# Modulation products of a two-block network: from TensorE column tiles to VectorE running sums

## The chip, the cores and the metric

One core of a Trainium2 chip. The metric is device time in microseconds (us) of one execution. Engines are named as in the profile: PE is TensorE (PEld its weight loads), DVE VectorE, ACT ScalarE, POOL GpSimd, SP the engine that issues the DMAs.

## The reference

Two transformer-like blocks of two layers each work on 256 context tokens and 256 latent tokens with 1024 features. Each layer l has a *modulation*: six vectors of 1024 numbers (shift, scale and gate for each half of the layer) for each of two conditions, c for the latent tokens and c_ctx for the context.

```python
def _modulation(cond, w, b):          # cond [1, 1024], w [1024, 6144]
    m = jax.nn.silu(cond) @ w + b
    return jnp.split(m[:, None, :], 6, axis=-1)

ml = _modulation(c, ada_w[i], ada_b[i])
mc = _modulation(c_ctx[None, :], ada_w[i], ada_b[i])
...
hl = _modulate(x, ml[0], ml[1])       # x * (1 + scale) + shift, latent tokens
...
x = _layer_norm(ALPHA * x + ml[2] * yl, ln_g[i, 0], ln_b[i, 0])
```

The context's stream ends in the last layer of each block, so that there only shift and scale of the first half (parts 0 and 1) are wanted for both conditions, and parts 2 to 5 for the latent condition alone. All data is fp32.

## The kernel before

Features lie on the 128 partitions and tokens in the columns. A projection takes its weights in chunks of 128x1024 fp32 (512 KB): `weight` (L266) loads a chunk into one of five buffers `raw`, ScalarE rounds it to `wh` (L280), VectorE, or GpSimd for each third chunk, subtracts to get the rest `wl` (L281), with three buffers for each of the two; `mm3` (L284) then issues three products for every 128x128 block (L286 to L288), of 512 columns where both halves of the tokens are worked on and of 256 where one is.

The program runs: first mixer (`_mlstm`), first feed-forward block (`_ffn`), attention mixer on the latent tokens (`_mla`), second feed-forward block, then the second block's mixers (`_mixers`) and MLPs (`_mlp`), twice. Between two of these stands a norm: `resid` (L478) adds the last products to the stream, `accumulate` gathers sums (L486 to L503), `token_sums` (L312) sums over partitions on TensorE, and `ln_stats`, `ln_rows`, `rsqrt` and `rows` (L512, L343, L344, L322 to L328, L352) make the statistics by a chain of small VectorE instructions of two to eight columns; L908 and L909 (or L928) then normalise tile by tile, and `split` (L263, L264) makes the pairs for the next products. In the stages with both halves of the tokens (`front`) the first products of the first half run while the second half's norm is made.

The modulations are not computed ahead, but in the background. `ada(l)` (L398) is a generator whose step loads one weight chunk and multiplies it; `later` (L431) queues it with a rate, and `tick` (L435), called by each `weight`, lets it do that many steps per weight chunk; `finish` (L446) runs what is left where the results are needed. Layer 0's last four parts run beside the first mixer, layer 1's and 2's beside the first feed-forward block and the attention mixer, layer 3's beside the first MLP: 22 parts of eight chunks, 176 in all. (Parts 0 and 1 of layer 0 have their own code, `first_mod`, at the start.)

A chunk holds 128 input features (partitions) by 1024 outputs. The conditions `cs` are the stationary operand, 128x32 of which two columns are not zero, and the chunk is the moving one, as four column tiles of 256 outputs side by side, summed over the eight chunks in one PSUM bank:

```python
for j in range(4):
    nc.tensor.matmul(ps[32 * j:32 * j + 32, 0:256], self.cs[:, l // 2, kt, :],
                     raw[:, j, :], start=(kt == 0), stop=(kt == KD - 1),
                     tile_position=(0, 32 * j))
```

Each of these fp32 products leaves two records in the trace, so a chunk is eight records of L411. After the eighth chunk ScalarE copies the bank (L417), TensorE transposes two blocks (L420) and VectorE adds the bias (L425).

The order in which each engine does its instructions is set when the program is built: a scheduler that keeps a timeline of its own places them, by their order in the code and by when it takes each to be ready. On the chip every engine works through its list in that order.

## Time and profile before

| | |
|---|---|
| Median of 3 runs | 2565.69 us (2559.06 to 2566.53) |
| Span of the profiled execution | 2551.4 us |
| PE busy | 2467.2 us, 97% |
| DVE busy | 1330.9 us, 52% |
| ACT busy | 1089.1 us, 43% |
| POOL busy | 629.9 us, 25% |

The span runs from the first to the last instruction of the profiled execution. That execution has no other time of its own on record; the runs are other executions, and their median lies 14.3 us above the span. Busy time is the time in which an engine had an instruction at work, overlaps counted once. Idle time of an engine costs nothing unless another waits for it.

### The profile page before, as it was taken

What the parts mean: (1) busy time and instruction counts of PE and PEld (TensorE: products, weight loads), DVE (VectorE), ACT (ScalarE), POOL (GpSimd) and SP (SyncE); (2) the same over time, 40 slices, a digit from 0 to 9 for tenths busy, and PEclk for the clock granted to TensorE, in tenths of its full rate; (3) what the DMA queues carried; (4) which work ended last, traced back from release to release, by engine and by line L of the source; (5) the groups of instructions that cost most, each with busy time, mean ns of one, the idle gap of its engine ahead of it and who ended that gap; (6) DMA issues with size and microseconds to landing.
All of it is one profiled execution on the core that took longest, in us unless ns stands there. A gap on an engine that the chain in (4) does not pass through costs nothing.

```text
span 2551.4 us, 38440 instructions
## 1 busy us (share of the span) xinstructions
PE 2467.2 (97%) x15258; PEld 2079.0 (81%) x15258; DVE 1330.9 (52%) x2412; ACT 1089.1 (43%) x1861; POOL 629.9 (25%) x447
## 2 busy tenths in 40 slices
PE   7999999999999999999999999899999999988998
PEld 5777877888898777778878999668877778977998
DVE  4613333533645333346766566886633334597665
ACT  4733233422434223235545556664522323475543
POOL 1111222221452111124022322542111112252222
PEclk9999999999999999999999999999999999998999
DMA  8555434533324455556357553123445555223554
GB/s 287 185 181 162 123 117 135 158 96 115 107 99 143 148 158 156 164 176 213 103 166 240 177 172 123 54 83 96 129 153 157 156 157 165 67 87 108 179 177 125
DMA packets 114758, 369.84 MB, mean 145 GB/s; under 512 B 12689, under 2 KB 17041, under 8 KB 114577
## 3 DMA queue, kind: packets, MB, share of 16 engines
q1 hardware_dynamic: 114576, 367.37, 45.7%
q8 instruction: 120, 1.97, 0.3%
q14 instruction: 62, 0.50, 0.1%
HBM read 357.88 MB, written 9.44 MB: 144 GB/s over the span
## 4 chain that ended last, share of the span: by engine, by line
PE 88%; DVE 6%; ACT 3%; DMA 2%; issue 1%; SPq 0%; POOL 0%; DVEq 0%; ACTq 0%
PE pm L286 24%; PE pm L288 23%; PE pm L287 23%; PE px L286 4%; PE pa L411 4%; PE px L287 4%; PE px L288 4%; DVE a L1395 1%; DVE wl L281 1%; DMA raw<-in_ada 1%; PE px L312 1%; PE pm L1137 1%; PE px L336 1%; ACT wh L280 0%; DVE a L264 0%
## 5 line engine op out<-in xcount | busy, mean ns | idle before, releaser
L286 PE MATMUL pm<-a,wh 128*128 128x512 f32 (+1 forms) x2432 | 847.3, 350 | 8.8 <-ACT a L263 3.0
L287 PE MATMUL pm<-a,wh 128*128 128x512 f32 (+1 forms) x2432 | 835.7, 344 | 0.0
L288 PE MATMUL pm<-a,wl 128*128 128x512 f32 (+1 forms) x2432 | 833.0, 344 | 0.8 <-DVE wl L281 0.7
L280 ACT CAST wh<-raw 128x1024 fp32r<-128x1024 f32 (+2 forms) x421 | 420.0, 1001 | 844.1 <-PE pm L287 471.3
L281 POOL TENSOR_TENSOR wl<-raw,wh 128x1024 fp32r<-128x1024 f32 (+2 forms) x140 | 321.7, 2298 | 1472.3 <-ACT wh L280 1434.8
L286 PEld LDWEIGHTS pm<-a,wh 128*128 128x128 f32 x2432 | 462.3, 191 | 103.4 <-issue 34.6
L281 DVE TENSOR_TENSOR wl<-raw,wh 128x1024 fp32r<-128x1024 f32 (+2 forms) x281 | 342.7, 1221 | 363.2 <-ACT wh L280 360.3
L288 PEld LDWEIGHTS pm<-a,wl 128*128 128x128 f32 x2432 | 461.8, 190 | 56.3 <-DVE wl L281 1.3
L287 PEld LDWEIGHTS pm<-a,wh 128*128 128x128 f32 x2432 | 463.4, 191 | 50.5 <-DVE a L909 0.8
L286 PE MATMUL pm<-a,a 128*128 128x256 f32 (+2 forms) x844 | 245.8, 298 | 6.8 <-ACT a L280 6.8
L287 PE MATMUL pm<-a,a 128*128 128x256 f32 (+2 forms) x844 | 247.6, 295 | 2.5 <-DVE a L264 1.6
L288 PE MATMUL pm<-a,a 128*128 128x256 f32 (+2 forms) x844 | 246.2, 294 | 0.0
L286 PEld LDWEIGHTS pm<-a,a 128*128 128x128 f32 x844 | 162.7, 195 | 17.0 <-ACT a L280 8.3
L478 DVE SCALAR_TENSOR_TENSOR a<-pm,mod,a 128x256 f32<-128x256 f32 x188 | 87.4, 480 | 164.3 <-PE pm L288 163.9
L287 PEld LDWEIGHTS pm<-a,a 128*128 128x128 f32 x844 | 163.9, 194 | 6.8 <-DVE a L264 2.2
L288 PEld LDWEIGHTS pm<-a,a 128*128 128x128 f32 x844 | 163.9, 194 | 3.3 <-issue 1.4
L263 ACT CAST a<-t 128x256 fp32r<-128x256 f32 (+2 forms) x173 | 86.3, 506 | 123.9 <-DVE t L1699 82.0
L264 DVE TENSOR_TENSOR a<-t,a 128x256 fp32r<-128x256 f32 (+2 forms) x173 | 110.1, 642 | 53.0 <-ACT a L263 51.2
L287 PE MATMUL pm<-wl,a 128*128 128x512 f32 (+1 forms) x336 | 130.2, 388 | 5.1 <-DVE wl L281 5.1
L286 PE MATMUL pm<-wh,a 128*128 128x512 f32 (+1 forms) x336 | 128.0, 383 | 1.5 <-ACT a L263 1.5
L288 PE MATMUL pm<-wh,a 128*128 128x512 f32 (+1 forms) x336 | 127.6, 386 | 0.0
L286 PE MATMUL px<-a,wh 128*128 128x256 f32 (+1 forms) x364 | 122.2, 337 | 0.0
(305 smaller groups left out, 3325.0 us busy)
## 6 DMA issues: line engine op xcount, KB each, us to landing
raw<-in_ada SPq DMA_DIRECT2D x192, 512.0 KB, 4.2
raw<-in_w_m SPq DMA_DIRECT2D x128, 512.0 KB, 3.6
raw<-in_ffn_in SPq DMA_DIRECT2D x88, 512.0 KB, 4.1
raw<-in_w_qk SPq DMA_DIRECT2D x32, 512.0 KB, 3.6
raw<-in_w_v SPq DMA_DIRECT2D x32, 512.0 KB, 3.6
raw<-in_ffn_oa SPq DMA_DIRECT2D x32, 512.0 KB, 4.1
raw<-in_w_inb SPq DMA_DIRECT2D x28, 512.0 KB, 3.6
raw<-in_w_up SPq DMA_DIRECT2D x16, 512.0 KB, 5.8
```

The costliest lines, as they stand in the source:

```text
L263: self.nc.scalar.copy(hi, src)
L264: self.nc.vector.tensor_sub(lo, src, hi.bitcast(F32))
L280: nc.scalar.copy(hi, raw)
L281: eng.tensor_sub(lo, raw, hi.bitcast(F32))
L286: mm(out, ah, bh, start=start, stop=False)
L287: mm(out, ah, bl, start=False, stop=False)
L288: mm(out, al, bh, start=False, stop=stop)
L312: self.nc.tensor.matmul(out_ps[:, i * nt + t:i * nt + t + 1], a[:, c0 + t * P:c0 + (t + 1) * P], self.ones[:, 0:1], start=(k == 0), stop=( ...
L336: self.nc.tensor.transpose(ps[:, t * P:(t + 1) * P], col[:, t:t + 1].to_broadcast([P, P]), self.ident)
L411: nc.tensor.matmul(ps[32 * j:32 * j + 32, 0:256], self.cs[:, l // 2, kt, :], raw[:, j, :], start=(kt == 0), stop=(kt == KD - 1), tile_posi ...
L478: self.nc.vector.scalar_tensor_tensor(z[:, a:b], ps[:, a:b], gate[:, kt, w:w + 1], z[:, a:b], op0=ALU.mult, op1=ALU.add)
L1137: nc.tensor.transpose(pt[:, s * P:(s + 1) * P], p[:, s * P:(s + 1) * P], K.ident)
```

## The change

`ada` no longer multiplies on TensorE chunk by chunk. It keeps, for each condition, an accumulator of 128x1024 fp32 in SBUF (from the activations' pool, which has 31 such buffers). Each chunk is multiplied by the condition's value on each partition and added: the first by ScalarE, the other seven by VectorE, once per condition. For parts 2 to 5 of layers 1 and 3 only the latent condition is summed, which makes 14 parts with two conditions and 8 with one. After the eighth chunk TensorE sums each accumulator over the partitions, by products with a matrix of ones on column tiles of 512 columns; then follow the copy, now four transposes instead of two, and the bias. The rate of layer 0's parts rises from 0.5 to 0.8 steps per weight chunk.

```diff
-    def ada(self, l, parts=range(6), mod=None):
+    def ada(self, l, parts=range(6)):
...
+        if l % 2:
+            nc.gpsimd.memset(mod, 0.0)
         yield mod
         bo = _PV["ada_b"][0] + 48 * l
         for part in parts:
-            ps = self.pa.tile([P, 512], F32, name=self.uid("pa"), tag="pa")
+            conds = (1,) if l % 2 and part > 1 else (0, 1)
+            nw = len(conds)
+            acc = [self.a4(F32, (P, D)) for _ in conds]
             for kt in range(KD):
-                raw = self.rawp.tile([P, 4, 256], F32, name=self.uid("raw"), tag="raw")
-                nc.sync.dma_start(raw, self.A["ada"][6 * l + part - 2, kt])
-                for j in range(4):
-                    nc.tensor.matmul(ps[32 * j:32 * j + 32, 0:256], self.cs[:, l // 2, kt, :],
-                                     raw[:, j, :], start=(kt == 0), stop=(kt == KD - 1),
-                                     tile_position=(0, 32 * j))
+                raw = self.rawp.tile([P, D], F32, name=self.uid("raw"), tag="raw")
+                nc.sync.dma_start(raw, self.A["ada"][6 * l + part - 2, kt].rearrange("p a b -> p (a b)"))
+                for s, w in zip(acc, conds):
+                    c = self.cs[:, l // 2, kt, w:w + 1]
+                    if kt == 0:
+                        nc.scalar.activation(s, raw, AF.Copy, scale=c)
+                    else:
+                        nc.vector.scalar_tensor_tensor(s, raw, c, s, op0=ALU.mult, op1=ALU.add)
                 if kt < KD - 1:
                     yield
+            ng = 32 * 2 * nw
+            ps = self.pa.tile([P, 512], F32, name=self.uid("pa"), tag="pa")
+            for i in range(2 * nw):
+                nc.tensor.matmul(ps[32 * i:32 * i + 32], self.ones[:, 0:32],
+                                 acc[i // 2][:, 512 * (i % 2):512 * (i % 2) + 512],
+                                 start=True, stop=True, tile_position=(0, 32 * i))
             rows = self.t2()
-            nc.scalar.copy(rows[:, 0:256], ps[:, 0:256])
+            nc.scalar.copy(rows[0:ng], ps[0:ng])
             pt = self.ax_ps()
-            for h in range(2):
-                nc.tensor.transpose(pt[:, h * P:(h + 1) * P], rows[:, h * P:(h + 1) * P], self.ident)
+            for t in range(4):
+                nc.tensor.transpose(pt[:, t * P:t * P + ng], rows[0:ng, t * P:(t + 1) * P], self.ident[0:ng, 0:ng])
...
-    K.later(rest, 0.5)
+    K.later(rest, 0.8)
```

The rest of the difference adds the bias by the new layout of the transposed block and takes comments out. Lines behind `ada` are 13 higher in the new program.

The new instructions move others, since the scheduler places all of them anew. Two places on VectorE's list matter below; every row there is one instruction, with its line, operation, output and inputs. The first is the norm at the start of the first feed-forward block, second half of the tokens, from the sums' scaling (`st`, L512) to the end of its statistics (L352). Before (`px` is the bank with the sums, `v` and `rs` the small tiles of the norm, `t` and `pm` hidden tiles and products of the feed-forward block):

```order
L512 TENSOR_SCALAR st_6006<-px_5997 128x4
L343 SCALAR_TENSOR_TENSOR v_6008<-st_6006 128x2
L344 SCALAR_TENSOR_TENSOR v_6008<-v_6008,st_6006 128x2
L322 TENSOR_SCALAR rs_6011<-v_6008 128x2
L365 SCALAR_TENSOR_TENSOR t_6197<-pm_6147,pv,t_6197 128x255
L323 TENSOR_TENSOR rs_6011<-rs_6011 128x2
L367 SCALAR_TENSOR_TENSOR t_6197<-pm_6147,pv,t_6197 128x255
L324 SCALAR_TENSOR_TENSOR rs_6011<-rs_6011,v_6008 128x2
L325 SCALAR_TENSOR_TENSOR rs_6011<-rs_6011 128x2
L326 SCALAR_TENSOR_TENSOR rs_6011<-rs_6011 128x2
L327 SCALAR_TENSOR_TENSOR rs_6011<-rs_6011 128x2
L328 SCALAR_TENSOR_TENSOR rs_6011<-rs_6011 128x2
```

With the change (L525 is L512 of before; `a_6056` and `a_6057` are accumulators of two conditions, `raw` the chunk, `cs` the conditions):

```order
L525 TENSOR_SCALAR st_5974<-px_5965 128x4
L281 TENSOR_TENSOR a_6093<-raw_6090,a_6092 128x1024
L420 SCALAR_TENSOR_TENSOR a_6056<-raw_6094,cs,a_6056 128x1024
L420 SCALAR_TENSOR_TENSOR a_6057<-raw_6094,cs,a_6057 128x1024
L365 SCALAR_TENSOR_TENSOR t_6163<-pm_6113,pv,t_6163 128x255
L343 SCALAR_TENSOR_TENSOR v_5976<-st_5974 128x2
L420 SCALAR_TENSOR_TENSOR a_6056<-raw_6104,cs,a_6056 128x1024
L420 SCALAR_TENSOR_TENSOR a_6057<-raw_6104,cs,a_6057 128x1024
L367 SCALAR_TENSOR_TENSOR t_6163<-pm_6113,pv,t_6163 128x255
L344 SCALAR_TENSOR_TENSOR v_5976<-v_5976,st_5974 128x2
L281 TENSOR_TENSOR wl_6465<-raw_6462,wh_6464 128x1024
L365 SCALAR_TENSOR_TENSOR t_6221<-pm_6171,pv,t_6221 128x255
```

Two additions stand behind the scaling and before each further step of the chain; ten of them lie between L525 and the norm's last statistic, which stands some rows further down, and a subtraction of a weight chunk (L281) that stood behind the norm now lies in it.

The second place is the norm at the end of the attention mixer, which has one half of the tokens only. Before:

```order
L512 TENSOR_SCALAR st_11154<-px_11141 128x4
L343 SCALAR_TENSOR_TENSOR v_11156<-st_11154 128x2
L344 SCALAR_TENSOR_TENSOR v_11156<-v_11156,st_11154 128x2
L322 TENSOR_SCALAR rs_11159<-v_11156 128x2
L323 TENSOR_TENSOR rs_11159<-rs_11159 128x2
L324 SCALAR_TENSOR_TENSOR rs_11159<-rs_11159,v_11156 128x2
L325 SCALAR_TENSOR_TENSOR rs_11159<-rs_11159 128x2
L326 SCALAR_TENSOR_TENSOR rs_11159<-rs_11159 128x2
L281 TENSOR_TENSOR wl_11325<-raw_11322,wh_11324 128x1024
L327 SCALAR_TENSOR_TENSOR rs_11159<-rs_11159 128x2
L328 SCALAR_TENSOR_TENSOR rs_11159<-rs_11159 128x2
L352 TENSOR_TENSOR st_11154<-st_11154,rs_11159 128x2
```

With the change:

```order
L525 TENSOR_SCALAR st_10994<-px_10981 128x4
L281 TENSOR_TENSOR wl_11155<-raw_11152,wh_11154 128x1024
L420 SCALAR_TENSOR_TENSOR a_10957<-raw_11156,cs,a_10957 128x1024
L420 SCALAR_TENSOR_TENSOR a_10958<-raw_11156,cs,a_10958 128x1024
L343 SCALAR_TENSOR_TENSOR v_10996<-st_10994 128x2
L420 SCALAR_TENSOR_TENSOR a_10957<-raw_11160,cs,a_10957 128x1024
L420 SCALAR_TENSOR_TENSOR a_10958<-raw_11160,cs,a_10958 128x1024
L344 SCALAR_TENSOR_TENSOR v_10996<-v_10996,st_10994 128x2
L420 SCALAR_TENSOR_TENSOR a_10957<-raw_11170,cs,a_10957 128x1024
L420 SCALAR_TENSOR_TENSOR a_10958<-raw_11170,cs,a_10958 128x1024
L322 TENSOR_SCALAR rs_10999<-v_10996 128x2
L420 SCALAR_TENSOR_TENSOR a_10957<-raw_11239,cs,a_10957 128x1024
```

Here, too, ten additions lie between the scaling and the last statistic, where one subtraction stood. From the second half's norm before the attention mixer to its first softmax (L1124 before, L1137 now) the list holds 28 additions, between that softmax and the last but one head none, and from there to the end of the norm just shown 28.

## Rows read from the trace of the kernel before

**Rows 1.** page, busy time by engine and the chain that ended last

```profile
PE 2467.2 (97%) x15258; PEld 2079.0 (81%) x15258; DVE 1330.9 (52%) x2412; ACT 1089.1 (43%) x1861; POOL 629.9 (25%) x447
...
PE 88%; DVE 6%; ACT 3%; DMA 2%; issue 1%; SPq 0%; POOL 0%; DVEq 0%; ACTq 0%
```

**Rows 2.** windows, L411 alone: stretch, width, busy us (records) of PE, PEld, clock, DMA

```profile
64.00:740.00 676.00, 21.87 (x256) 5.64 (x256) 1.00 0.45 136
740.00:1080.00 340.00, 26.66 (x344) 8.29 (x344) 1.00 0.47 147
1080.00:1400.00 320.00, 35.15 (x432) 10.19 (x424) 0.98 0.54 180
1400.00:2200.00 800.00, 30.05 (x384) 7.85 (x384) 0.98 0.43 133
1160.00:1250.00 90.00, 11.69 (x144) 3.57 (x144) 1.00 0.58 199
1290.00:1350.00 60.00, 9.84 (x96) 2.28 (x96) 0.89 0.66 215
```

**Rows 3.** timeline of PE around one chunk: start us, us, instruction

```profile
111.21 0.39 PE L287 MATMUL pm<-a,wh 128*128 128x512 f32 x1
111.44 0.39 PE L288 MATMUL pm<-a,wl 128*128 128x512 f32 x1
111.75 0.64 PE L411 MATMUL pa<-raw,cs 128*32 128x256 f32 x8
...
112.66 0.39 PE L287 MATMUL pm<-a,wh 128*128 128x512 f32 x1
```

**Rows 4.** timeline of PE around two chunks in a row

```profile
1102.81 0.39 PE L288 MATMUL pm<-a,wl 128*128 128x512 f32 x1
1103.12 1.07 PE L411 MATMUL pa<-raw,cs 128*32 128x256 f32 x16
...
1104.47 0.40 PE L287 MATMUL pm<-a,wh 128*128 128x512 f32 x1
```

**Rows 5.** timeline of PE around the two transposes of a part

```profile
164.40 0.39 PE L288 MATMUL pm<-a,wl 128*128 128x512 f32 x1
...
165.08 0.39 PE L287 MATMUL pm<-a,wh 128*128 128x512 f32 x1
```

**Rows 6.** groups by line: DVE L365 (min/median/max ns), L281, L1395, ACT L280 (busy, mean)

```profile
L365 DVE SCALAR_TENSOR_TENSOR t<-pm,pv,t x60: 471/742/750, 69.2 to 1526.5; 128x510 f32<-128x510 f32 x32, 128x255 f32<-128x255 f32 x28
...
L281 DVE TENSOR_TENSOR a<-raw,a 128x1024 fp32r<-128x1024 f32 x34 | 50.1, 1480 | 11.7 <-ACT a L280 10.5 <-issue 0.5 <-DMA hf<-in_xT 0.5
...
L1395 DVE SCALAR_TENSOR_TENSOR a<-a,pv,a 128x512 f32<-128x512 f32 x30 | 32.3, 1088 | 0.2
...
L280 ACT CAST wh<-raw 128x1024 fp32r<-128x1024 f32 (+2 forms) x421 | 420.0, 1001 | 844.1 <-PE pm L287 471.3
```

**Rows 7.** timeline of DVE at the first feed-forward block's norm

```profile
767.47 0.16 DVE L512 TENSOR_SCALAR st<-px 128x4 f32<-128x4 f32 x1
...
771.89 0.16 DVE L352 TENSOR_TENSOR st<-st,rs 128x2 f32<-128x2 f32 x1
771.97 1.23 DVE L281 TENSOR_TENSOR wl<-raw,wh 128x1024 fp32r<-128x1024 f32 x1
773.11 0.42 DVE L1061 TENSOR_TENSOR t<-t,pm 128x256 f32<-128x256 f32 x1
```

**Rows 8.** windows, all engines: busy us (records) of PE, PEld, DVE, ACT, POOL, clock

```profile
1600.00:1664.00 64.00, 52.60 (x235) 40.59 (x235) 61.05 (x83) 38.62 (x70) 35.77 (x21) 0.89 0.22 74
...
1160.00:1250.00 90.00, 87.96 (x697) 74.91 (x696) 65.76 (x160) 53.07 (x110) 29.44 (x26) 1.00 0.58 199
...
1290.00:1350.00 60.00, 54.66 (x419) 43.98 (x418) 40.78 (x90) 30.58 (x64) 23.98 (x25) 0.89 0.66 215
...
768.00:788.00 20.00, 20.00 (x168) 19.09 (x161) 19.37 (x46) 15.61 (x29) 10.28 (x10) 1.00 0.59 196
1790.00:1810.00 20.00, 16.75 (x126) 15.20 (x127) 19.14 (x37) 17.27 (x35) 5.26 (x3) 0.91 0.74 252
```

More of the change, by code (lines that the diff above doesn't have):

```diff
@@ L395, in first_mod @@
                                     op0=ALU.add, op1=ALU.add)
-    def ada(self, l, parts=range(6), mod=None):
+    def ada(self, l, parts=range(6)):
         nc = self.nc
-        if mod is None:
-            mod = self.cp.tile([P, 6, KD, 2], F32, name=f"mod{l}", tag=f"mod{l}")
+        mod = self.cp.tile([P, 6, KD, 2], F32, name=f"mod{l}", tag=f"mod{l}")
+        if l % 2:
+            nc.gpsimd.memset(mod, 0.0)
         yield mod
@@ L418, in ada @@
             pt = self.ax_ps()
-            for h in range(2):
-                nc.tensor.transpose(pt[:, h * P:(h + 1) * P], rows[:, h * P:(h + 1) * P], self.ident)
-            m = mod[:, part].rearrange("p (j h) w -> p h j w", h=2)
-            b = self.pv[:, bo + part * KD:bo + (part + 1) * KD].rearrange("p (j h) -> p h j", h=2)
-            t = pt[:, 0:256].rearrange("p (h j w) -> p h j w", h=2, j=4)
-            for h in range(2):
-                nc.vector.tensor_tensor(m[:, h], t[:, h, :, 0:2],
-                                        b[:, h].unsqueeze(2).to_broadcast([P, 4, 2]), op=ALU.add)
+            for t in range(4):
+                nc.tensor.transpose(pt[:, t * P:t * P + ng], rows[0:ng, t * P:(t + 1) * P], self.ident[0:ng, 0:ng])
@@ L427, in ada @@
+            m = mod[:, part].rearrange("p (h t) w -> p w h t", h=2)
+            b = self.pv[:, bo + part * KD:bo + (part + 1) * KD].rearrange("p (h t) -> p h t", h=2)
+            t = pt.rearrange("p (t w h c) -> p w h t c", t=4, w=2, h=2)
+            for i, w in enumerate(conds):
+                nc.vector.tensor_tensor(m[:, w], t[:, i, :, :, 0], b, op=ALU.add)
             if part in (1, 4):
```

## The prediction

> **What bounds the kernel now.** I read the page first: TensorE is busy for 97% of a span of 2551.4 us and holds 88% of the chain that ended last, VectorE 6% [rows 1]. The reader should see that a microsecond taken from TensorE's queue shortens the span wherever nothing else is late, and that VectorE, at 52% overall, has room on average. An average says nothing of a stage, so I next cut the span into stages and counted the modulation products (records of L411, eight to a weight chunk) in each: 32 chunks beside the first mixer, 43 in the first feed-forward block, 54 from its end through the attention mixer into the second feed-forward block (one of them is cut by the boundary and counted twice), 48 in the last MLP stage that has them [rows 2]. Then the timeline of TensorE around single chunks [rows 3 to 5], because overlapping records make the busy time of a group less than what it costs. Last the busy time of VectorE in the stretches where the new order puts the added work [rows 8].
>
> **What TensorE loses and gains.** Products of L287 and L288 start 0.23 us apart. With one chunk between them L287 starts at 112.66 instead of about 111.90 [rows 3]: a chunk costs 0.77 us, more than the 0.57 us until the next product starts. Two chunks in a row cost 104.47 - 103.27 = 1.20 us, so the second adds 0.43 us [rows 4]. TensorE's order before has 155 groups: 113 of one chunk (87 us), 23 of two (28 us), and 19 pieces that hold the other 17 chunks (13 us at 0.77). Together **128 us, 0.73 us a chunk**.
>
> Added are 72 products that sum over partitions, in 24 groups of two or four column tiles. No row shows a 512-column fp32 product on a column tile. From below, one such group costs as much as a chunk, 0.77 us, if length were free; from above, as two chunks issued apart, 1.54 us. I take 0.77 plus the 0.43 us that 256 further columns cost in rows 4, so 1.20 us, 29 us in all. Two transposes cost 165.08 - 164.86 = 0.22 us [rows 5]; there are now four per part, 22 parts, 5 us more. So 34 us come back, 1.5 us a part, and TensorE's queue is **94 us** shorter. Bounds with the two prices: 104 and 86 us.
>
> **What VectorE gets.** 252 SCALAR_TENSOR_TENSOR of 128x1024: 14 parts with two conditions and 8 with one, seven chunks each (the eighth is 36 scaled copies on ScalarE, at nothing: ScalarE is busy for 43% of the span and holds 3% of the chain [rows 1]; a cast of that size took 1.0 us [rows 6], so without that cover they cost 36 us). The trace has none of 1024 columns. The same operation takes 0.471 us at 255 columns and about 0.745 at 510 [rows 6], which continued gives 1.29 us. An instruction of 1.23 us is followed by the next start after 1.14 us [rows 7], so one occupies the engine for **1.20 us**. The lower bound is that 1.14 us of a 1024-column subtraction; the upper is the same operation beside GpSimd, 1.088 us at 512 columns instead of 0.745 [rows 6], which scaled is 1.75 us. I take 1.20, since GpSimd was busy for a third to two fifths of the two stretches that count most [rows 8]. The whole is 302 us of VectorE.
>
> The DMAs are the same 176 chunks of 512 KB and I cost them at nothing; their buffers come free when VectorE, not TensorE, has read them. Raising the rate from 0.5 to 0.8 steps a chunk in the first mixer only packs the four parts there closer. Each accumulator takes one of 31 buffers of the activations' pool, at nothing as long as no allocation in the first mixer waits for it; that cover is the earlier finish of these parts.
>
> **By stage.**
> - First mixer: 32 chunks give 23 us, four parts take 6: **-17**. VectorE is idle for much of that stage.
> - First feed-forward block: 43 chunks give 31, five parts take 8. At its start VectorE is busy for 19.4 of 20 us [rows 8], and the second half of TensorE's front products waits for the norm made there. The new order puts ten of the added instructions between L512 and L352 of that norm, which in the trace ran from 767.47 to 771.89 [rows 7]: 12 us later, less 1 us for the chunks that stood there. **-12**.
> - Attention: in two stretches the order puts 28 instructions each, from the second half of the norm to the first softmax (1160 to 1250) and from the last heads to the final norm of the mixer (1290 to 1350). VectorE's 65.8 + 28 x 1.20 = 99.4 us must fit into 90, and 40.8 + 33.6 = 74.4 into 60 [rows 8]. The fullest stretch of the trace reaches 95% [rows 8], which makes 104.6 and 78.3: **+14.6 and +18.3**. The 30 chunks that TensorE no longer does there [rows 2] give nothing, since VectorE sets the pace. The other 24 chunks of the stage give 17.5, three parts take 4.5: the stage is **+20**.
> - MLP stage: 48 chunks give 35, six parts take 9. At its start VectorE is at 19.1 of 20 us [rows 8] and gets ten more instructions before the last tile of the norm; TensorE has front products of the first half as cover for about half of the 12 us, so 6 come back: **-20**.
>
> In the stretch from 1290 to 1350 the granted clock was 0.89, so TensorE fell from its 2.4 GHz level to 1.2 for part of it, after it had waited [rows 8]; I cost further falls at nothing, because VectorE is then late anyway. The Trainium skill (TensorE: Matmul & The Clock Gate, Why this matters for your kernels) says that idle gaps between bursts of products drop the clock to half rate, which speaks against a change that makes TensorE wait; by it, the same share lost in 90 us of the first stretch would add 10 us.
>
> Sum: -17 - 12 + 20 - 20 = about **-30 us** on the span of 2551.4. The median of the runs, 2565.7, is 14.3 us above the span, which I take as unchanged: 2565.7 - 30 = **2535 us**.
>
> **Rivals.**
> - *Everything is covered* (faster still). VectorE had 48% idle, and if the added instructions fell only into its waits, all 94 us would be gained: **2472**. For it: TensorE was busy for 98% of the first of the two stretches, part of that with chunks as filler; VectorE's waits there, 24 of 90 us, nearly hold 33.6 us. Against it: they do not hold it, and the norm's small instructions are a chain. Chance 0.24.
> - *The change does not do what it says*: VectorE's additions are late in the dense stages too, by their place in the queue before L281 of the weights, and what TensorE gives up returns as waits for `wl`. Price: 30 us of waits over the other 146 chunks, 0.2 us each, makes it **2565**. Against it: three weight buffers keep such subtractions some 10 us ahead where a chunk of weights takes TensorE 24 x 0.23 = 5.4 us. Chance 0.12.
> - *The instruction is dearer* (slower). Mechanism: each addition reads two operands in SBUF, and in the trace such instructions grow beside GpSimd: the subtraction of 1024 columns took 1.48 us in the mean where it kept its weights, against 1.23 alone [rows 6, 7]. 56 instructions at 95% use, ten at the start of the feed-forward block and five uncovered at the MLP are worth 74 of full price. At 1.75 us they cost 74 x 0.55 = 41 us more: **2576**. It decides from 1.61 us on (30 / 74 = 0.41 above 1.20); for 0.3% slower, 1.71 us. Against it: the 1.75 comes from a convolution that VectorE shares with GpSimd, busy there for 35.8 of 64 us [rows 8]. Chance 0.14. The Trainium skill (SBUF — State Buffer, Who interferes with whom) has the rule: a VectorE instruction with two SBUF inputs contends with a GpSimd instruction that reads SBUF, and the later one blocks; the rows agree as far as they go.
>
> **How the numbers follow.** The forecast has 0.50, with its own range 2505 to 2560. About 0.3% (8 us) is what a measurement of this kernel can tell from no change. Faster by more: 0.24 of full cover and 0.45 of the forecast, **0.69**. Within: 0.05 of the forecast and the 0.12 of the second rival, **0.17**. Slower: **0.14**. The range of 8 in 10 goes from **2478**, leaving out the ends of full cover, to **2572**, leaving out the dearer half of the third rival; the bounds of the sum products (8 us) lie inside.
>
> **What would show it.** Right: no L411 in TensorE's rows; 252 additions of 1.2 to 1.35 us; VectorE at 95% or more from the norm before the attention mixer to its first softmax and again at the mixer's end, TensorE idle there with VectorE named; the stage from the end of the first feed-forward block to the second longer by 10 to 30 us, the other three shorter by 12 to 20 each. Wrong: TensorE still at 97% in the attention stage (then full cover); additions of 1.6 us or more; or waits for `wl` spread over the dense stages.

## The result, and the profile after

The change makes the kernel slower. The median of four runs is **2603.86 us** (2603.36 to 2606.06), against 2563.37 us (2559.06 to 2566.53) for four runs of the kernel before: a ratio of **1.0165 [1.0145, 1.0185]** (the two medians alone give 1.0158). The forecast was 2535 us, with a range that ended at 2572.

The profiled execution of the new kernel spans 2601.8 us, 50.4 more than that of before. The medians differ by 40.5 only: in the new kernel's runs the span lies 1.9 us below the time, so the execution of before with its span of 2551.4 was one of the fast ones (its times begin at 2559.06), and not, as the prediction took it, one 14.3 us below its own time. The differences by stage below add up to 50.4 us, so they are some 10 us too large in sum.

The page first, engines and the chain of work that ended last, which answer to [rows 1]:

```profile
PE 2421.3 (93%) x14038; PEld 2091.6 (80%) x14038; DVE 1660.9 (64%) x2656; ACT 1128.3 (43%) x1897; POOL 672.7 (26%) x449
...
PE 75%; DVE 13%; DMA 4%; ACT 3%; issue 3%; POOL 1%; SPq 0%; DVEq 0%; ACTq 0%; POOLq 0%
```

TensorE's busy time fell by 46 us where its queue was to be 94 shorter, and it stands idle for 180 us instead of 84. VectorE's share of the chain has doubled.

To find the place, both traces are cut where TensorE has issued the same number of its other products. Without the modulation both programs have 13,806 of them, and the cuts below lie at 3600, 4000, 5200, 7200, 8800, 9200 and 11200: up to the end of the first mixer, the front of the first feed-forward block, the rest of it, the attention stage (into the second feed-forward block), the rest of that and some of the second mixers, the end of the first of these, and the MLP with layer 3's modulation. Windows of the kernel before (stretch, width, busy us and records of PE, PEld, DVE, ACT, POOL, then PE's clock, DMA share, GB/s):

```profile
0.00:751.50 751.50, 734.76 (x3865) 594.20 (x3866) 295.20 (x514) 283.94 (x461) 177.14 (x140) 1.00 0.47 147
751.50:807.10 55.60, 55.60 (x451) 51.16 (x450) 36.30 (x78) 29.00 (x54) 21.87 (x22) 1.00 0.43 143
807.10:1109.70 302.60, 302.60 (x1531) 231.26 (x1530) 111.43 (x152) 86.05 (x106) 38.39 (x16) 1.00 0.51 156
1109.70:1432.30 322.60, 312.66 (x2416) 271.10 (x2416) 203.83 (x432) 161.97 (x307) 93.27 (x77) 0.98 0.54 181
...
1668.40:1756.80 88.40, 82.03 (x403) 64.21 (x402) 72.85 (x164) 59.04 (x111) 29.70 (x24) 0.94 0.22 65
1756.80:2177.70 420.90, 414.62 (x2397) 333.55 (x2396) 179.44 (x292) 134.39 (x213) 69.90 (x42) 0.99 0.48 150
```

The same work in the changed kernel:

```profile
0.00:753.20 753.20, 722.11 (x3649) 594.71 (x3650) 378.07 (x570) 292.43 (x469) 186.14 (x142) 0.99 0.45 147
753.20:823.00 69.80, 59.44 (x411) 54.56 (x410) 54.69 (x92) 31.85 (x56) 24.15 (x22) 0.88 0.40 129
823.00:1102.50 279.50, 279.50 (x1241) 226.97 (x1240) 165.94 (x191) 92.62 (x112) 40.03 (x16) 1.00 0.51 168
1102.50:1491.70 389.20, 318.13 (x2081) 281.44 (x2081) 311.70 (x515) 174.59 (x319) 121.35 (x77) 0.91 0.46 148
...
1728.60:1826.20 97.60, 84.66 (x403) 65.89 (x402) 75.85 (x169) 60.98 (x115) 30.92 (x25) 0.90 0.25 74
1826.20:2225.70 399.50, 388.92 (x2059) 330.48 (x2057) 242.69 (x339) 140.97 (x216) 71.22 (x41) 0.98 0.47 155
```

| Stage | before | after | difference | predicted |
|---|---|---|---|---|
| to the end of the first mixer | 751.5 | 753.2 | +1.7 | -17 |
| front of the feed-forward block | 55.6 | 69.8 | +14.2 | -12 (with the next row) |
| rest of the feed-forward block | 302.6 | 279.5 | -23.1 | |
| attention stage | 322.6 | 389.2 | **+66.6** | **+20** |
| end of a second mixer | 88.4 | 97.6 | +9.2 | 0 |
| MLP with layer 3 | 420.9 | 399.5 | -21.4 | -20 |
| the two stretches left out above | 609.8 | 613.0 | +3.2 | 0 |

The reader should see two things. Where TensorE is dense (823 to 1102.5) it stays at 100% and at full clock, and the stage is shorter by what the products cost. In the attention stage it has 335 records less and is yet busy for 5.5 us longer, at a mean clock of 0.91, that is for longer at its 1.2 GHz level; and it is idle for 71 us instead of 10. VectorE is busy for 80% of it. The forecast had 95% for two stretches of the stage alone, 1160 to 1250 and 1290 to 1350 us in the trace of before; the same products lie here in the changed kernel:

```profile
1158.10:1276.70 118.60, 94.15 (x580) 80.82 (x580) 100.70 (x197) 56.33 (x112) 40.37 (x24) 0.90 0.46 142
1316.80:1398.90 82.10, 53.11 (x342) 45.33 (x341) 74.66 (x115) 34.03 (x67) 28.06 (x24) 0.79 0.54 176
```

VectorE was busy there for 100.7 and 74.7 us, as worked out ahead (99.4 and 74.4), but that is 85% and 91%. The two stretches grew by 28.5 and 22.1 us. The rest of the stage grew by 16.0, and holds the other 28 of the stage's 84 additions.

How an addition gets into the way is best read where the attention stage begins. Timeline of VectorE (start us, us, instruction): the statistics of the next norm (L1129, L322) and the pairs of the latent tokens (L921, L922, L264) alternate with additions two at a time, in the order of its list.

```profile
1196.70 1.27 DVE L420 SCALAR_TENSOR_TENSOR a<-raw,cs,a 128x1024 f32<-128x1024 f32 x1
1197.90 0.15 DVE L1129 TENSOR_SCALAR v<-px 128x2 f32<-128x2 f32 x1
1197.97 1.43 DVE L420 SCALAR_TENSOR_TENSOR a<-raw,cs,a 128x1024 f32<-128x1024 f32 x1
...
1199.98 0.41 DVE L264 TENSOR_TENSOR a<-hf,a 128x256 fp32r<-128x256 f32 x1
1200.32 1.27 DVE L420 SCALAR_TENSOR_TENSOR a<-raw,cs,a 128x1024 f32<-128x1024 f32 x1
1201.51 0.15 DVE L322 TENSOR_SCALAR rs<-v 128x2 int32<-128x2 int32 x1
1201.58 1.27 DVE L420 SCALAR_TENSOR_TENSOR a<-raw,cs,a 128x1024 f32<-128x1024 f32 x1
...
1203.44 0.41 DVE L264 TENSOR_TENSOR a<-hf,a 128x256 fp32r<-128x256 f32 x1
```

TensorE, in the same microseconds, waits each time for the pair behind the two additions (in brackets idle us and what ended it):

```profile
1200.45 0.39 PE L287 MATMUL pm<-a,a 128*128 128x256 f32 x1 [1.66 <-DVE a L264]
...
1203.90 0.38 PE L287 MATMUL pm<-a,a 128*128 128x256 f32 x1 [1.76 <-DVE a L264]
...
1207.37 0.39 PE L287 MATMUL pm<-a,a 128*128 128x256 f32 x1 [1.78 <-DVE a L264]
```

The group of the additions by form over the whole run, beside the rows that priced it ahead [rows 6, 7]:

```profile
L420 DVE SCALAR_TENSOR_TENSOR a<-raw,cs,a 128x1024 f32<-128x1024 f32 x252 | 365.0, 1471 | 140.4 <-DMA raw<-in_ada 137.6
```

One took 1471 ns in the mean (the shortest 1260, the median 1280), and VectorE stood before them for 137.6 us because a chunk had not landed. The prediction had nothing for that wait.

### The profile page after: what moved, and what is told of

The parts are those of the page before. It is cut to its first block, busy times and chain, and to the rows that moved or that the text cites. A ratio compares the mean times of both kernels' runs of the same rounds, so it can differ in the third digit from the quotient of the medians.

```text
span 2601.8 us, 36381 instructions
## 1 busy us (share of the span) xinstructions
PE 2421.3 (93%) x14038; PEld 2091.6 (80%) x14038; DVE 1660.9 (64%) x2656; ACT 1128.3 (43%) x1897; POOL 672.7 (26%) x449
## 4 chain that ended last, share of the span: by engine, by line
PE 75%; DVE 13%; DMA 4%; ACT 3%; issue 3%; POOL 1%; SPq 0%; DVEq 0%; ACTq 0%; POOLq 0%
PE pm L286 20%; PE pm L288 20%; PE pm L287 20%; PE px L286 3%; PE px L287 3%; PE px L288 3%; DVE a L420 3%; DVE wl L281 2%; DMA raw<-in_ada 2%; DVE a L1408 1%; DVE a L264 1%; PE pa L427 1%; PE px L312 1%; ACT wh L280 1%; DVE a L281 1%
## 5 line engine op out<-in xcount | busy, mean ns | idle before, releaser
L288 PE MATMUL pm<-a,wl 128*128 128x512 f32 (+1 forms) x2432 | 840.2, 347 | 14.3 <-DVE wl L281 12.0
L287 PE MATMUL pm<-a,wh 128*128 128x512 f32 (+1 forms) x2432 | 841.8, 347 | 0.0
L280 ACT CAST wh<-raw 128x1024 fp32r<-128x1024 f32 (+2 forms) x421 | 420.3, 1001 | 749.0 <-PE pm L287 397.0
L281 POOL TENSOR_TENSOR wl<-raw,wh 128x1024 fp32r<-128x1024 f32 (+2 forms) x140 | 334.9, 2392 | 1432.1 <-ACT wh L280 1356.7
L286 PEld LDWEIGHTS pm<-a,wh 128*128 128x128 f32 x2432 | 468.6, 193 | 90.8 <-ACT wh L280 16.7
L288 PEld LDWEIGHTS pm<-a,wl 128*128 128x128 f32 x2432 | 468.2, 193 | 72.4 <-DVE wl L281 15.0
L287 PEld LDWEIGHTS pm<-a,wh 128*128 128x128 f32 x2432 | 469.7, 193 | 53.1 <-issue 1.6
L281 DVE TENSOR_TENSOR wl<-raw,wh 128x1024 fp32r<-128x1024 f32 (+2 forms) x281 | 345.3, 1231 | 199.1 <-ACT wh L280 197.3
L420 DVE SCALAR_TENSOR_TENSOR a<-raw,cs,a 128x1024 f32<-128x1024 f32 x252 | 365.0, 1471 | 140.4 <-DMA raw<-in_ada 137.6
L287 PE MATMUL pm<-a,a 128*128 128x256 f32 (+2 forms) x844 | 252.2, 301 | 10.6 <-DVE a L264 9.7
L286 PE MATMUL pm<-a,a 128*128 128x256 f32 (+2 forms) x844 | 248.6, 306 | 14.3 <-ACT a L280 3.6
L288 PE MATMUL pm<-a,a 128*128 128x256 f32 (+2 forms) x844 | 250.4, 300 | 1.9 <-DVE a L281 1.8
L286 PEld LDWEIGHTS pm<-a,a 128*128 128x128 f32 x844 | 167.3, 202 | 21.8 <-ACT a L263 5.6
L287 PEld LDWEIGHTS pm<-a,a 128*128 128x128 f32 x844 | 169.3, 201 | 15.3 <-DVE a L264 11.6
L288 PEld LDWEIGHTS pm<-a,a 128*128 128x128 f32 x844 | 168.9, 201 | 5.1 <-DVE a L281 2.9
L287 PE MATMUL pm<-wl,a 128*128 128x512 f32 (+1 forms) x336 | 131.1, 390 | 5.1 <-DVE wl L281 5.1
L264 DVE TENSOR_TENSOR a<-t,a 128x256 fp32r<-128x256 f32 (+2 forms) x173 | 110.0, 642 | 36.7 <-ACT a L263 34.6
```

What stands on the lines that cost most here:

```text
L264: self.nc.vector.tensor_sub(lo, src, hi.bitcast(F32))
L280: nc.scalar.copy(hi, raw)
L281: eng.tensor_sub(lo, raw, hi.bitcast(F32))
L286: mm(out, ah, bh, start=start, stop=False)
L287: mm(out, ah, bl, start=False, stop=False)
L288: mm(out, al, bh, start=False, stop=stop)
```

## Experiments

Theory *place*: an addition costs nothing where TensorE is dense and VectorE has time, and its whole duration in the attention stage, where TensorE keeps needing VectorE's next result. Rivals: *price* (the instruction is dearer than estimated, wherever it stands), *late chunks* (VectorE's list stands still for DMAs), and *sums* (TensorE's own queue stands at the sum products). In each comparison the kernel before ran again: 2558.9 to 2560.5 us in the median.

### One generator back on TensorE, or alone on VectorE

Here `ada_pe` is the `ada` of the kernel before.

```diff
-        gen2 = K.ada(2, (1, 0, 2, 4, 3, 5))
+        gen2 = K.ada_pe(2, (1, 0, 2, 4, 3, 5))
```

> Layer 2's modulation (the six parts whose additions fall from the end of the first feed-forward block to the start of the second) goes back to TensorE's column tiles; layers 0, 1 and 3 stay with VectorE. Theory 'place': counted along TensorE's other products, the changed kernel lost 66.7 us in the attention stage (from product 5200 to 7200), where VectorE has no room, and gained or lost little elsewhere: +1.7 to the end of the first mixer, -8.9 in the first feed-forward block, -9 behind the attention stage. Then this kernel gives 2563 + 1.7 - 8.9 - 9 = about 2547 us, 2538 to 2556, faster than both. Rival 'price': an addition costs the same everywhere, the +41 us are 252 additions at 0.16 us net each; then 168 additions leave 2563 + 27 = 2590 us.

Measured: **2542.3 us**, 0.9932 [0.9908, 0.9956] of before. With the additions of layer 2 alone on VectorE (`ada` for layer 2, `ada_pe` for 0, 1 and 3):

> Only layer 2's modulation is summed by VectorE, the other parts by TensorE as before (and the first mixer's rate is 0.5 again). Theory 'place': the whole loss of the attention stage stays, 2563 + 60 to 70 = 2623 to 2633 us, slower than the changed kernel itself. Rival 'price': 84 of 252 additions, 2563 + 14 = 2577 us.

Measured: **2636.1 us**, 1.0300 [1.0284, 1.0315]: 84 additions cost more than all 252. *Price* falls by 48 us in the one run and by 59 in the other, and *place* holds to 5 us and, in the second run, to 3 us beyond its range. In the same attention stretch the first of the two shows VectorE at its old load and TensorE nearly as before:

```profile
1101.60:1431.70 330.10, 317.41 (x2406) 272.46 (x2405) 202.73 (x431) 161.81 (x307) 91.41 (x77) 0.97 0.51 174
```

### VectorE's time, or the chunks it waits for

```diff
-nc.vector.scalar_tensor_tensor(s, raw, c, s, ...)
+nc.vector.scalar_tensor_tensor(s[:, 0:2], raw[:, 0:2], c, s[:, 0:2], ...)
```

> Each of VectorE's 252 additions works on 2 of the 1024 columns: the chunk is loaded and waited for as in the changed kernel, TensorE sums over partitions as there, but VectorE's time for the additions (365 us busy) is left out, and most of the sum with it. Theory 'load': the loss is VectorE's time in the attention stage; without it nearly all of TensorE's 94 us come through, 2470 to 2490 us. Rival 'late chunks': VectorE, which waited 137.6 us for chunks in its in-order list, and TensorE's sum products, which waited 43.9 us for additions, lose the time by waiting for the DMAs; then this kernel stays above 2560 us.

Measured: **2510.1 us**, 0.9800 [0.9782, 0.9818]: between the two. VectorE's time is worth 94 us of the 2604, but 114 or more were expected. Windows of this kernel, of the dense part and of the attention stage:

```profile
801.90:1081.50 279.60, 279.60 (x1241) 227.21 (x1241) 119.07 (x191) 93.03 (x112) 38.32 (x16) 1.00 0.49 168
1081.50:1403.20 321.70, 295.91 (x2082) 269.63 (x2081) 222.95 (x515) 175.08 (x319) 91.49 (x77) 0.96 0.52 178
```

The dense part takes 279.6 us, and took 279.5 with whole additions: there 47 us of VectorE's time cost nothing. The attention stage takes 321.7 us, and took 322.6 before: with hardly any of VectorE's load, and 50 chunks less on TensorE, it is as long as before. (VectorE's list still waits for the chunks there, 16.6 us in this trace.)

The other half of the question, additions without chunks:

```diff
-raw = self.rawp.tile(...); nc.sync.dma_start(raw, ...)
+if kt == 0: raw = self.rawp.tile(...); nc.sync.dma_start(raw, ...)
...
-nc.vector.scalar_tensor_tensor(s, raw, c, s, ...)
+nc.vector.scalar_tensor_tensor(s, s, c, s, ...)
```

> Seven of eight chunk loads are left out, and each addition reads its own accumulator in place of the chunk: VectorE has the same 252 additions of 128x1024, but none waits for a DMA, and 154 chunks less pass through the five load buffers. Theory 'load': the attention stage stays as slow, and only the stall of the first mixer (PE idle for 6.3 us at 208, then half clock for 6.8 us) and its like go, 2580 to 2600 us. Rival 'late chunks': 2500 to 2530 us.

Measured: **2589.2 us**, 1.0111 [1.0094, 1.0129], as *load* had it. The attention stage lasts as long as in the changed kernel, 392.2 us, though seven of eight modulation chunks are not loaded:

```profile
1087.90:1480.10 392.20, 323.06 (x2082) 283.00 (x2081) 310.96 (x515) 175.32 (x319) 122.61 (x77) 0.89 0.28 90
```

What late chunks do cost lies in the first mixer. In the changed kernel VectorE stood for 6.28 us at an addition whose chunk came late, with the rest of a weight chunk (`wl`) behind it:

```profile
209.30 3.93 DVE L420 SCALAR_TENSOR_TENSOR a<-raw,cs,a 128x1024 f32<-128x1024 f32 x2 [6.28 <-DMA raw<-in_ada]
213.16 2.35 DVE L281 TENSOR_TENSOR wl<-raw,wh 128x1024 fp32r<-128x1024 f32 x2
```

TensorE, next, waited for that `wl` and then ran products at 0.43 us instead of 0.23 for a while. Without the chunk loads (products 800 to 1200) the stretch is 12.0 us shorter; the changed kernel's row was

```profile
159.30:267.20 107.90, 97.31 (x426) 76.48 (x425) 58.38 (x59) 35.00 (x44) 12.93 (x5) 0.97 0.54 176
```

and this kernel's is

```profile
158.80:254.70 95.90, 93.62 (x426) 75.18 (x426) 51.93 (x55) 35.22 (x44) 12.95 (x5) 1.00 0.40 134
```

The rate has a part in that:

```diff
-    K.later(rest, 0.8)
+    K.later(rest, 0.5)
```

> The changed kernel with the first mixer's rate at 0.5 steps again. Theory 'rate': the chunks come late for VectorE at 173 and 208 us because 0.8 steps per weight chunk press them into fewer load buffers; then the 12 us that the kernel without chunk loads gained there come back, 2588 to 2594 us. Rival: the stall comes from the order on VectorE, whatever the rate: 2600 to 2608 us.

Measured: **2597.8 us**, 1.0134 [1.0111, 1.0157]: 6 us less than the changed kernel, between the two expectations, and with intervals that overlap, so the time alone settles nothing. Its trace does: the same stretch takes 95.9 us, as without chunk loads, so at this place the old rate takes the stall away. The rate alone does not make it, though: in the kernel with additions of two columns, at the new rate and with all loads, the stretch takes 97.4 us, where the kernel before took 96.9.

```profile
160.10:257.50 97.40, 95.12 (x425) 76.34 (x424) 32.03 (x53) 35.12 (x44) 12.59 (x5) 0.98 0.53 176
```

It takes both, packed chunks and whole additions. Four of the 12 us that the old rate gains are lost again further on, and the first stage lasts 745.1 us instead of 753.2.

### How the cost grows

```diff
...
-            conds = (1,) if l % 2 and part > 1 else (0, 1)
+            conds = (1,) if l == 2 or l % 2 and part > 1 else (0, 1)
```

> Layer 2's context condition is left out: the same 48 chunks are loaded, but VectorE adds for one condition, 42 additions in place of 84, and TensorE sums half as much. Counted along its other products, the changed kernel lost 66.7 us net in the attention stage while some 52 chunks (38 us, less 9 for sums and transposes) left TensorE there: gross 96 us for 80 additions, 1.2 us each. Theory 'VectorE is the path there': each addition left out gives back its 1.2 us, 40 x 1.2 = 48 and a little of sums, so 2604 - 50 = 2554 us, 2545 to 2565. Rival 'threshold': VectorE has room for 40 additions and is late only for the second 40; then all 96 us come back, about 2510 us.

Measured: **2555.8 us**, 0.9976 [0.9967, 0.9986]: 48.1 us come back for 42 additions and the sums that go with them, **1.15 us each**, nearly their duration. The threshold falls. The attention stage gives three points: 321.7 us with additions of two columns, 345.2 with 42 whole ones, 389.2 with 84.

```profile
1101.40:1446.60 345.20, 301.97 (x2058) 272.42 (x2057) 257.85 (x467) 168.89 (x313) 107.10 (x77) 0.94 0.50 166
```

The first 42 cost 23.5 us, or 0.56 each, the second 42 cost 44.0, or 1.05 each. So a good part of the first was hidden, and little of the second.

A rival that no run was made for is the order: the scheduler gave every version an order of its own in this stage. The traces on record bound it. With 84 whole additions the stage took 389.2 to 398.6 us in five orders (the changed kernel, layer 2 alone, and the versions without chunk loads, with free sums and with the old rate), without additions and with 48 or 50 chunks on TensorE 322.6 to 330.1 us in three (before, layer 2 back on TensorE, and the first of the faster versions below). Order and execution together move it by up to some 10 us: far less than 66.6, but enough to make the split of 0.56 and 1.05 a rough one.

### GpSimd for half of them

```diff
+                    elif l == 2 and w == 0:
+                        t = self.a4(F32, (P, D))
+                        nc.scalar.activation(t, raw, AF.Copy, scale=c)
+                        nc.gpsimd.tensor_add(s, s, t)
```

> For layer 2's context condition ScalarE makes the product and GpSimd adds it (42 additions of 128x1024 move from VectorE to GpSimd); the rest as in the changed kernel. If the additions cost only as VectorE's time, this is as fast as the kernel that leaves the 42 out, 2554 us, plus a few us, 2550 to 2570. Rival 'contention': a GpSimd addition of about 2.4 us holds up VectorE's instructions with two operands in SBUF beside it; in the changed kernel an addition that GpSimd's work overlapped in part took 2.05 us in the mean instead of 1.28. At 0.8 us for each of 42, and GpSimd's own norm additions late behind them, 2590 us or more.

Measured: **2639.0 us**, 1.0304 [1.0289, 1.0320]: *contention* holds, and beyond its lower bound by 49 us. The kernel that leaves these additions out is 83 us faster. Groups by form, 1102 to 1530 us, VectorE:

```profile
L424 DVE SCALAR_TENSOR_TENSOR a<-raw,cs,a 128x1024 f32<-128x1024 f32 x42 | 82.0, 1951 | 12.4 <-DMA raw<-in_ada 8.9 <-ACT a L418 3.2
L281 DVE TENSOR_TENSOR wl<-raw,wh 128x1024 fp32r<-128x1024 f32 x22 | 39.7, 1810 | 12.1 <-ACT wh L280 12.1
```

and GpSimd:

```profile
L422 POOL TENSOR_TENSOR a<-a,a 128x1024 f32<-128x1024 f32 x42 | 114.8, 2735 | 117.2 <-ACT a L421 116.4
```

VectorE's remaining additions took 1.95 us instead of 1.46 in the kernel with these 42 alone, its subtractions 1.81, and its load in the stage did not fall at all (314.3 us, against 311.7 with 84 additions and 257.8 where the 42 are left out). The Trainium skill (SBUF — State Buffer, Who interferes with whom) has it that a VectorE instruction with two SBUF inputs and a GpSimd instruction that reads SBUF block one another; this trace agrees with 1951 ns against 1280. How much of the 83 us is VectorE's slowness and how much the waiting for GpSimd's own results was not separated.

### The sum products

```diff
-acc[i // 2][:, 512 * (i % 2):512 * (i % 2) + 512],
+self.pv[:, 0:512],
```

> TensorE's sum products read a constant in place of the accumulators, so they wait for no addition (all additions are still made; the sums are left out of the result). Theory 'sums block TensorE': the 43.9 us that its queue stood at these products, and the half clock behind (23.9 us at 1367), go: 2604 - 44 - 10 = about 2550 us. Rival 'chain': at the two norms the statistics that TensorE needs next stand behind the same additions on VectorE, so the wait moves to the next product of the norm and little is gained: 2590 to 2604 us.

Measured: **2600.5 us**, 1.0165 [1.0136, 1.0193]: as *chain* had it. At the end of the attention mixer the changed kernel's sum product had waited 20.39 us, and the norm's own chain (L325 to L352) ended 1.7 us later still:

```profile
1386.95 3.02 PE L427 MATMUL pa<-a,hm 128*32 128x512 f32 x8 [20.39 <-DVE a L420]
1389.91 0.69 PE L336 MATMUL px<-cst,rs 128*128 128x128 f32 x2
```

With the wait taken away, TensorE waits there for the norm's statistic instead, 20.8 us at the longest (waits in its attention stage: line waited for, us, times, longest):

```profile
PE px L336 <- DVE rs L328: 25.2, 2, 20.8
```

### What TensorE's relief was worth there

```diff
+                for j in range(4 if l == 2 else 0):
+                    nc.tensor.matmul(ps[32 * j:32 * j + 32, 0:256], self.cs[:, l // 2, kt, :],
+                                     raw[:, 256 * j:256 * j + 256], ...)
```

> The changed kernel, and for layer 2 TensorE's chunk products as before on top (their result is overwritten by the sums): the 48 chunks that the change took off TensorE there come back, the additions stay. Theory 'TensorE waits there anyway': in the attention stage it was idle for 71 us in the changed kernel, and 48 x 0.73 = 35 us of products go into these waits (and hold its clock up): 2604 us, 2595 to 2612, so its relief was worth nothing there. Rival 'TensorE still sets the pace between its waits': 2604 + 35 = 2639 us, 2625 or more.

Measured: **2613.7 us**, 1.0211 [1.0196, 1.0226]: 10 us more than the changed kernel for 48 chunks that were priced at 35, just above the range of the first theory and 11 below the least that the rival allows. The attention stage itself grew by 5.6 us (394.8), less than a new order can move it. With the additions in place, most of the products that come back go into TensorE's waits, so to take them off was worth at most about a third of their price.

### Versions that beat both

All of layer 2 and the first parts of layers 1 and 3 by the code of before, rate 0.5:

```diff
         for part in parts:
+            if l == 2 or l % 2 and part == 0:
...
+                continue
```

(The branch holds the code of before.)

> TensorE keeps layer 2's modulation and the first parts of layers 1 and 3 (those that run where a feed-forward or MLP stage begins); the first mixer's rate is 0.5; the other 14 parts are VectorE's (140 additions). Stage by stage, against the kernel before: first mixer -6 (as with rate 0.5), first feed-forward block -20 (the loss of 14 us at its start gone, eight chunks back on TensorE), attention +7 and second mixers +6 (as with layer 2 on TensorE), last MLP stage -21: 2560 - 34 = 2526 us, 2518 to 2534. Rival 'front': the 14 us at the start of the feed-forward block come from something else than the additions in the norm there; then 2540 us, no better than with layer 2 alone on TensorE.

Measured: **2517.0 us**, 0.9838 [0.9823, 0.9852]: 1.6% faster than before and, by the two ratios, 3.2% faster than the change; it is 1 us below the forecast's range. The front of the feed-forward block is back at its old length, so the 14 us there came with that part; additions of two columns, with the same loads and sums, had left 58.5 of 69.8 us, so 11 of the 14 are VectorE's time in the norm:

```profile
744.60:800.70 56.10, 55.81 (x451) 51.19 (x450) 36.80 (x78) 29.20 (x54) 21.86 (x22) 1.00 0.42 141
```

Two attempts to give VectorE more, in places where it has room, gained nothing further. Starting layers 1 and 2 in the first mixer:

```diff
-    K.later(rest, 0.8)
+    K.later(rest, 0.5)
+    K.later(K.gens[0], 0.7)
+    K.later(K.gens[1], 0.8)
...
```

(`K.gens` holds the generators of layers 1 and 2. A switch, not shown, gives TensorE each part of them that begins at the start of the feed-forward block or in the attention stage, and the first part of layer 3.)

> The modulations of layers 1 and 2 start behind layer 0's in the first mixer (rates 0.5, 0.7, 0.8), so that VectorE adds them where it was busy for some 24 of 64 us, and is not given them at the start of the feed-forward block or in the attention stage: there TensorE multiplies the chunks that are left (18 of layer 2's, and eight of layer 3's first part). VectorE has 210 additions for 150 chunks. Theory 'place': 150 chunks give TensorE 150 x 0.73 = 110 us, sums and transposes of 19 parts cost 29, stalls on late chunks and at the stages' starts some 10 to 15: 2560 - 67 = about 2493 us, 2480 to 2510. Rival 'price': each addition costs the time that it costs on the mean in the changed kernel wherever it stands (41 us for 252): 2590 us. Rival 'buffers': two accumulators and a chunk taken from the mixer's buffers make its own work wait: above 2520 us.

Measured: **2520.8 us**, 0.9851 [0.9834, 0.9867], 28 us above the forecast. Its trace has three parts, 24 chunks, on TensorE (the expectation counted 26). The sums of the others now stand in a mixer that has no more products to lose for them: the first stage takes 756.6 us, 12.0 more than in the version above. From product 400 to 3600 TensorE is busy 7.5 us longer there, with ten more sum products, and idle 3.5 us longer. So the rival *buffers*, whose time (above 2520 us) fits, explains at most the smaller part by waits. The attention stage gives back 4 (321.8 against 325.8). And two more parts in the first feed-forward block, layer 1 at rate 1.2:

```diff
-            if l == 2 or l % 2 and part == 0:
+            if l == 2 and part not in (1, 0) or l % 2 and part == 0:
```

> As the version with 140 additions, but layer 1's rate is 1.2 instead of 0.8 and the first two parts of layer 2 are VectorE's too, so that 16 more chunks are added in the first feed-forward block, where VectorE has room, and TensorE's products of layer 2's other parts come earlier. Theory 'place': 16 chunks give 12 us, two parts' sums take 3, and nothing is added in the attention stage: 2517 - 9 = 2508 us, 2498 to 2514. Rival: TensorE's chunk products in the attention stage only filled waits there, and in the dense block each costs its 0.73 us: the 14 moved there cost 10 us, 2517 to 2522.

Measured: **2520.0 us**, 0.9843 [0.9826, 0.9859]: the rival's time, but not its mechanism. The attention stage, with 20 chunks and one part's sums less on TensorE and no addition more, falls to 315.4 us, 10.4 below the version with 140 additions: some 0.5 us a chunk, so there the products did not only fill waits (the order can have a part in it). The two stretches of the feed-forward block grow from 336.7 us to 353.3, and not by 14 chunks that moved there, since TensorE has only four more in them (12 for 8). The front grew by 9.1 us, as VectorE got 12 additions at the norm again, and the dense part by 7.5, with two chunks and ten sum products more:

```profile
746.50:811.70 65.20, 58.86 (x468) 53.37 (x467) 48.45 (x92) 31.51 (x56) 24.37 (x22) 0.95 0.57 194
811.70:1099.80 288.10, 287.19 (x1302) 228.64 (x1301) 190.56 (x211) 95.68 (x116) 38.69 (x16) 1.00 0.57 188
```

## Why the prediction was wrong

**Right: TensorE's prices.** 43 chunks at 0.73 us less five groups of sums and transposes were to give 23 us, and the dense part of the feed-forward block, which has most of them, is 23.1 us shorter. One group of two sum products, priced at 1.20 us, takes 1.18: behind it L287 starts at 940.79 us where 939.61 was due. A group of four, for which the prediction had the same price, takes 1.19 (890.15 us instead of 888.96). The MLP stage came out at -21.4 for -20, with 2.5 us lost near its start (products 9600 to 9700) where 6 were put down. The front of the feed-forward block cost 14.2 us, where 12 less 1 were worked out for it.

**Right: the instruction's duration.** 1.29 us was read off [rows 6]; alone it takes 1.28: that is the mean of the 172 additions that no GpSimd instruction overlapped. The other 80 took 1.89 in the mean. (The instruction of [rows 6] reads one operand from a PSUM bank, `pm`, and the addition none; that its line led to the right size was in part luck.) The third rival (1.75 us, 2576 us) had the mechanism, but not the size: the mean of all is 1.47, and in the attention stage (1102 to 1440 us) it is 1.415, which makes (1.415 - 1.28) x 80 = 11 us there.

**Wrong: the attention term, +20, which was +66.6.** This step failed: "VectorE's 65.8 + 28 x 1.20 = 99.4 us must fit into 90 ... The fullest stretch of the trace reaches 95%". The load was right (100.7 and 74.7 us), the share was not: VectorE filled 85% and 91% of the two stretches, and they cost 28.5 and 22.1 us instead of 14.6 and 18.3, which is 18 of the 46.6 us that were missing. The step counts an addition only where VectorE is full. But 95% came from a stretch (1600 to 1664 us) where 26.6 of VectorE's 61 busy us are a convolution's running sums (L1395), before which it stood idle for 0.2 us in all. In the attention stage norms, heads and pairs go between VectorE, ScalarE and TensorE and back, and VectorE's idle time lay between the steps of these chains (23.6 of its 24 idle us from 1160 to 1250, before, were waits for results of the other two); an addition put there is done in the idle time only if it ends before the next step is ready. At 80% busy the stage was already nearly as slow as if each of the last 42 additions stood in the path whole: 1.05 us for each in the stage.

**Wrong in the same term: "The other 24 chunks of the stage give 17.5, three parts take 4.5".** The rest of the stage was to become 13 us shorter by that, and became 16.0 longer: the other 29 of the 46.6 us. There, too, stand 28 additions, 14 ahead of the first stretch (+5.2 us) and 14 behind the second (+10.5), and the prediction put them at nothing without a reason; between the two stretches, where no addition stands, the time is the same to 0.3 us. The chunks' price was wrong there as well. Putting 48 chunks back cost 10 us in place of 35, and with hardly any load on VectorE the stage was as long as before, though a version without additions there and with 20 chunks less was 10.4 us shorter. TensorE was busy for 312.7 of 322.6 us there (and in the two pieces of [rows 8] for 98% and 91%), but a part of the products went where it would otherwise have waited. A busy engine was taken for a bound one.

**Wrong: "I cost further falls at nothing, because VectorE is then late anyway"** (falls of TensorE's clock). In the stage the mean clock fell from 0.98 to 0.91, and TensorE was busy longer with less work. The Trainium skill (TensorE: Matmul & The Clock Gate, Why this matters for your kernels) warns of just this, that gaps between bursts drop the clock to half, and the trace agrees with those numbers. How much of the 66.6 us the clock alone makes no run separated from the waits that cause it. An estimate from the two traces: TensorE was busy at the 1.2 GHz level for 47.9 us of the stage, before for 9.5, and a product of 512 columns took 0.43 us at that level for 0.23 at full clock (first mixer, at 215 us), so these 38 us more would be some 18 less at full clock.

**Wrong: the first mixer, -17, which was +1.7.** The step was "The DMAs are the same ... and I cost them at nothing". They are the same, but a late chunk stopped one group of products on TensorE before, and now stops VectorE's whole list, `wl` of the dense stage with it. Leaving the loads out gave 12.0 us in one stretch, so did the old rate, and additions of two columns gave 10.5; "only packs the four parts there closer" was the second half of the error. That is the second rival's mechanism (waits for `wl`), at one place instead of spread. Some 3 us of the rest come ahead of the first addition (at 95.8 us): by the first 400 products every kernel run here lay 2.6 to 7.1 us behind the profiled execution of before.

**Wrong: nothing outside the modulations' stages.** The end of a second mixer, where no chunk is handled, took 9.2 us longer. TensorE's order there has a transposition (L1150) that waits 7.2 us for the softmax (L1585). Six of the variants lost 5 to 11 us there, three 3 to 4 and three under 2, with nothing in their edits that touches the place. The traces point to the scheduler's order: from product 9000 to 9200 no version has TensorE's order of before, which took 37.0 us (the changed kernel 46.2); three versions that share one order took 39.7 to 39.9, two that share another 38.5 each, two that share a third 43.8 and 47.6. The prediction put a new order outside the two places that it read at nothing.

## What to carry to other kernels

Room on an in-order engine is not its idle share: ask of each gap whether the work put into it ends before the next instruction that another engine waits for. Work moved off the bound engine pays where that engine is dense; where it waits on the receiver of the work, the relief is worth little and the new load counts nearly in full. Moving only the parts that fall into dense stages gave 1.6% where moving all cost as much.

## What was not expected of the hardware

GpSimd's additions of 128x1024 took 2.74 us, and slowed VectorE's two-operand instructions beside them from 1.28 to 1.95 us (additions) and from 1.23 to 1.81 (subtractions), so that sharing the work did not lighten VectorE's stage. And TensorE, after the wait of 20.39 us at the end of the attention mixer, had a granted clock of 0.50 (its 1.2 GHz level) for the sum products behind it. Four of them took 3.02 us, where four at full clock took 1.06. Not all of that is the clock: a record of these products took 1.06 us here for 0.60 there, and the second two came after the last addition, which ended at 1388.00 us. The window over them, and the four at full clock:

```profile
1386.90:1390.00 3.10, 3.05 (x9) 0.50 (x10) 1.69 (x6) 0.00 (x0) 0.00 (x0) 0.50 0.42 114
...
888.82 1.06 PE L427 MATMUL pa<-a,hm 128*32 128x512 f32 x8
```

The first row is a window of the changed kernel, in the columns of the windows above; the second is a row of its timeline.
